# Attention scores as two fp32r passes over stacked halves, the residual parked in HBM, and transposes at later places

## The chip, the cores and the metric

The kernel runs on one core of a Trainium2 chip: TensorE (matrix products and transposes, PE in the profile, its weight loads PEld), VectorE (DVE), ScalarE (ACT), GpSimd (POOL), SyncE (SP), whose queue asks for the transfers, and 16 DMA engines. The metric is the time of one execution on the device in microseconds, as the median of several runs. A profile of one such execution shows every instruction of every engine; its time is counted over the span from its first to its last instruction.

## The reference

One layer of a decoder on 512 tokens of width 1024, all in fp32: two half-step SwiGLU feed-forward blocks, and between them a mixer in which a gated delta rule (four heads of 128) and a differential attention (four heads, two softmax maps of 64 dimensions each) stand side by side. Cut to what matters here:

```python
x = layer_norm(alpha * x + 0.5 * swiglu_ffn(x, ffn1_w13, ffn1_w2), ln1_g, ln1_b)
h = x @ w_in
gq, gk, gv, gz, ga, gb, dq, dk, dv = jnp.split(h, offsets, axis=-1)
y_a = gdn_mixer(gq, gk, gv, gz, ga, gb, ...)       # chunked delta rule, then RMS norm and a silu gate
y_b = diff_attention_mixer(dq, dk, dv, ...)
x = layer_norm(alpha * x + concatenate([y_a, y_b]) @ w_out, ln2_g, ln2_b)
ple = sigmoid(x @ ple_gate_w) * (p @ ple_proj_w)
x = layer_norm(alpha * x + 0.5 * swiglu_ffn(x, ffn2_w13, ffn2_w2) + ple, ln3_g, ln3_b)

# differential attention, one block of 128 queries
s = einsum("bqhmd,bkhmd->bhmqk", qb, k) * scale    # m: the two maps, d: 64
pr = softmax(where(q_pos >= k_pos, s, -inf))
attn = pr[:, :, 0] - lam * pr[:, :, 1]
y = rms_norm(einsum("bhqk,bkhd->bqhd", attn, v), subln_w) * (1 - lam_init)
```

## The kernel before

**Tiling.** The 512 tokens are four row blocks of 128, t = 0 to 3. The residual x lives in four tiles RES[t] of 128x1024 with tokens on the partitions; its transposed form, with the 1024 features on the partitions, is kept twice: XH, rounded to the narrower format fp32r, and XL, what the rounding left. Every weight is split in the same way, by a ScalarE cast (line 159) and a VectorE subtract (line 160). A product is then three fp32r passes, high by high, low by high and high by low (`mm3`, lines 297 to 299).

**First feed-forward block.** `ffn` ends (lines 604 to 624) with the second product of the last group, per row block t and half j. `natural(t)` is then the layer norm of the block (`norm_natural`, lines 302 to 334): statistics and most of the scaling on VectorE, the last 256 columns scaled by ScalarE and GpSimd (line 326 is GpSimd's last step). `norm_turn(t)` (lines 336 to 344) makes XH and XL of the block by eight transposes on TensorE. `turn(t - 1)` follows `natural(t)`; block 3 is turned within the next stage.

**Mixers.** `mix_zone` opens with values and gates, and the keys and queries of the delta rule. Then it weaves generators ("lanes"). Each yields a pair: the nominal TensorE cost of what it has just put into the program, and the time to wait before its next step; `weave` lets the first lane go on whose time has come. So the nominal numbers set the order of the program; a scheduler then sets that of each engine's queue, and every engine works its queue off in order. The lanes are: `gdn(c)`, the delta rule's inner work on four chunks; `diagonal`; `chain`, the state carried over the chunks; sixteen `attention(t, h)`, of which two are in flight at a time; `fill`, dense products (the attention's keys and queries and the remaining values and gates z) that stand between the others; `out_attn` and `out_gdn`, the output projection of either half of the mix.

**Attention.** `fill` makes the rotated keys and queries in natural form, transposes them (`turn4`, line 871) and a VectorE copy puts them into DKT and DQT, fp32 tiles with the 4 x 128 head dimensions on the partitions. A head (lines 1147 to 1188) then makes, for each of two maps, an fp32 product of 64 rows (line 1159), adds the causal mask by a bf16 product (line 1160), takes the row maximum (1161), the exponential (1164), weighs and adds the maps (1168), transposes the result (1172), copies it (1174), multiplies it with the values DV (1178) and norms the rows (1181 to 1186). Its result overwrites its queries in DQT; `to_mix` transposes it and splits it into XH and XL.

**Chain.** For each chunk, TensorE makes products with the state ST (lines 1205 and 1213), VectorE the new values (1207), TensorE a triangular solve's product (1220), ScalarE copies it (1222), TensorE the state's change (1230) and the output (1238), VectorE adds them (1235, 1241), ScalarE squares (1247), and VectorE scales four heads (1252).

**After the mixers.** `out_gdn` adds the projection to RES, norms each block and turns the one before; the second feed-forward stage (`second_ffn`) begins with the gate of the layer embedding and turns block 3 ahead of its t = 2.

## Time and profile before

| | us |
|---|---|
| median of 3 runs (1098.52 to 1100.03) | 1098.65 |
| the profiled execution | 1099.23 |
| its span, first to last instruction | 1097.4 |
| TensorE busy | 1068.6 (97%) |
| VectorE busy | 828.2 (75%) |
| ScalarE busy | 489.9 (45%) |
| GpSimd busy | 112.9 (10%) |

The span has these stretches: the first feed-forward block to 340 us, the norm and turn of its rows to 366, values, keys and queries to 478, the woven delta rule and attention heads to 612, chain and output projection to 667, its norms and turns to 700, and the second feed-forward block. A busy share is a mean over stretches with different limits, so each stretch is to be read by itself. A bracket behind a row of the timeline gives how long the engine stood before it, and what it had waited for. Matmuls are pipelined and their ends are modelled: the time that one takes in a row of many is read from start to start.

### The profile page before, as it was taken

The page shows a single profiled execution, that of the slowest core. Times are in us where ns is not written, and L with a number is a line of the kernel's source. Part 1 is how long each engine was busy: PE and PEld are TensorE (multiplying, and loading weights), DVE is VectorE, ACT ScalarE, POOL GpSimd, SP SyncE. Part 2 cuts the span into 40 slices and gives each one's busy share as a digit, 9 for nine tenths or more (in the row PEclk, how much of TensorE's full clock was granted, in tenths as well). Part 3 has the DMA queues.
Part 4 walks back from the last instruction along what each step waited for, and adds up shares of the span by engine and source line. Part 5 has one row for each costly group of instructions (what it writes and reads, how often), then busy time and mean ns, then how long its engine had stood idle before and what let it go on. Part 6 is the DMA issues. An engine that isn't in the chain of part 4 may idle for free.

```text
span 1097.4 us, 17374 instructions
## 1 busy us (share of the span) xinstructions
PE 1068.6 (97%) x6627; PEld 939.8 (86%) x6627; DVE 828.2 (75%) x1446; ACT 489.9 (45%) x948; POOL 112.9 (10%) x175
## 2 busy tenths in 40 slices
PE   9999999999999989999999999999999999999996
PEld 7889898989897978778865887779899998999895
DVE  5989796979678366356665658889989696979568
ACT  5745353535333356324365533545544353535231
POOL 1100000000002202432112213100000000000003
PEclk9999999999999999999999999999999999999999
DMA  8633332433242042123210201524343332433212
GB/s 293 202 110 116 103 109 77 117 107 104 77 136 77 1 135 80 36 78 87 58 39 20 77 16 62 163 87 135 101 131 97 106 106 78 118 112 97 77 39 96
DMA packets 44275, 106.03 MB, mean 97 GB/s; under 512 B 10848, under 2 KB 12528, under 8 KB 44192
## 3 DMA queue, kind: packets, MB, share of 16 engines
q1 hardware_dynamic: 37968, 96.71, 29.0%
q0 software_dynamic: 1808, 6.04, 1.7%
q10 hardware_dynamic: 4416, 2.16, 0.7%
q8 instruction: 52, 0.85, 0.3%
q14 instruction: 31, 0.25, 0.1%
HBM read 102.41 MB, written 2.49 MB: 96 GB/s over the span
## 4 chain that ended last, share of the span: by engine, by line
PE 55%; DVE 5%; POOL 2%; DMA 2%; ACT 2%; issue 1%; DVEq 0%; SPq 0%; ACTq 0%; POOLq 0%
PE pb L297 9%; PE pb L298 9%; PE pb L299 9%; PE pc L298 4%; PE pc L299 4%; PE pc L297 4%; PE pa L299 3%; PE pa L298 3%; PE pa L297 3%; PE pc L1159 2%; DMA raw<-in_wa_dram 2%; DVE wl L160 2%; ACT wh L159 1%; PE pa L1092 1%; PE pc L1178 1%
## 5 line engine op out<-in xcount | busy, mean ns | idle before, releaser
L160 DVE TENSOR_TENSOR wl<-raw,wh 128x1024 fp32r<-128x1024 f32 (+3 forms) x137 | 144.2, 1058 | 37.6 <-ACT wh L159 36.4
L159 ACT CAST wh<-raw 128x1024 fp32r<-128x1024 f32 (+3 forms) x137 | 123.2, 906 | 96.7 <-PE pa L298 30.7
L297 PE MATMUL pb<-wh,hh 128*128 128x512 f32 (+1 forms) x356 | 138.3, 389 | 3.7 <-DVE RES L807 1.5
L298 PE MATMUL pb<-wl,hh 128*128 128x512 f32 (+1 forms) x356 | 138.1, 388 | 0.0
L299 PE MATMUL pb<-wh,hl 128*128 128x512 f32 (+1 forms) x356 | 137.8, 387 | 0.0
L229 ACT CAST th<-tr 128x512 fp32r<-128x512 f32 x160 | 98.7, 620 | 83.4 <-PE pc L298 48.2
L233 DVE TENSOR_TENSOR tl<-tr,th 128x512 fp32r<-128x512 f32 x160 | 109.7, 687 | 11.0 <-ACT th L229 10.2
L190 ACT CAST wh<-raw 128x512 fp32r<-128x512 f32 x88 | 54.6, 623 | 135.1 <-PE pb L299 90.8
L297 PE MATMUL pb<-wh,XH 128*128 128x512 f32 (+2 forms) x288 | 110.8, 385 | 2.2 <-ACT wh L159 0.6
L298 PE MATMUL pb<-wl,XH 128*128 128x512 f32 (+2 forms) x288 | 106.1, 369 | 1.0 <-DVE wl L160 0.9
L299 PE MATMUL pb<-wh,XL 128*128 128x512 f32 (+2 forms) x288 | 105.9, 368 | 0.0
L298 PE MATMUL pa<-XL,wh 128*128 128x256 f32 (+1 forms) x344 | 100.0, 291 | 0.2 <-DVE XL L160 0.2
L297 PE MATMUL pa<-XH,wh 128*128 128x256 f32 (+1 forms) x344 | 100.0, 291 | 0.2 <-ACT wh L159 0.2
L299 PE MATMUL pa<-XH,wl 128*128 128x256 f32 (+1 forms) x344 | 99.9, 290 | 0.0
L297 PE MATMUL pc<-XH,th 128*128 128x256 f32 x320 | 90.6, 283 | 0.0
L298 PE MATMUL pc<-XL,th 128*128 128x256 f32 x320 | 90.6, 283 | 0.0
L299 PE MATMUL pc<-XH,tl 128*128 128x256 f32 x320 | 90.6, 283 | 0.0
L490 DVE TENSOR_TENSOR RES<-RES,pb 128x512 f32<-128x512 f32 (+1 forms) x81 | 54.6, 677 | 45.1 <-PE pb L299 44.4
L191 DVE TENSOR_TENSOR wl<-raw,wh 128x512 fp32r<-128x512 f32 x88 | 60.2, 691 | 32.2 <-ACT wh L190 32.0
L297 PEld LDWEIGHTS pb<-wh,hh 128*128 128x128 f32 x356 | 66.9, 188 | 19.4 <-DVE RES L807 1.8
L299 PEld LDWEIGHTS pb<-wh,hl 128*128 128x128 f32 x356 | 66.9, 188 | 13.7
L298 PEld LDWEIGHTS pb<-wl,hh 128*128 128x128 f32 x356 | 66.9, 188 | 13.2 <-DVE wl L191 0.3
(303 smaller groups left out, 2639.8 us busy)
## 6 DMA issues: line engine op xcount, KB each, us to landing
raw<-in_wa_dram SPq DMA_DIRECT2D x127, 512.0 KB, 3.7
raw<-in_wb_dram SPq DMA_DIRECT2D x88, 256.0 KB, 2.7
raw<-in_wd_dram SPq DMA_DIRECT2D x4, 520.0 KB, 3.7
RES<-in_xn_dram POOLq DMA_DIRECT2D x4, 512.0 KB, 6.3
gb<-in_gb_dram POOLq DMA_DIRECT2D x8, 256.0 KB, 3.9
xr<-in_xT_dram ACTq DMA_DIRECT2D x7, 256.0 KB, 4.4
out_dram<-RES SPq DMA_DIRECT2D x5, 256.0 KB, 2.1
TT<-in_gb_dram POOLq DMA_DIRECT2D x4, 256.0 KB, 3.6
```

Of the source, the lines that this page charges most:

```text
L159: return (self.nc.scalar.copy(hi, src), self.nc.vector.tensor_tensor(lo, src, hi.bitcast(F32), ALU.subtract))
L160: self.nc.vector.tensor_tensor(lo, src, hi.bitcast(F32), ALU.subtract))
L190: nc.scalar.copy(hi, r)
L191: nc.vector.tensor_tensor(lo, r, hi.bitcast(F32), ALU.subtract)
L229: act.copy(h, t)
L233: dve.tensor_tensor(hl[1], t, hl[0].bitcast(F32), ALU.subtract)
L297: pe.matmul(o, wh, xh, start=first, stop=False)
L298: pe.matmul(o, wh, xl, start=False, stop=False)
L299: pe.matmul(o, wl, xh, start=False, stop=last)
L490: dve.tensor_tensor(rj, rj, pd, ALU.add)
L1092: pe.matmul(pt[:, h * P:(h + 1) * P], MP[:, 0, c, h, :], TT[:, c, h, :], start=True, stop=True)
L1159: pe.matmul(sc[m], DQT[r, h, t * P:(t + 1) * P], DKT[r, h, 0:n], start=True, stop=False)
```

## The change

**Scores.** Keys are split. Each map m gets a tile KK[:, m] of 128 rows: the 64 rows of its own hold the high part of its keys, the 64 others the low part. A head first prepares its queries in a slot of QZ (four slots, used in turn): the high part of map m's queries on both halves of the rows, and a padded tile with their low part on the map's own rows and zeros on the others (zeroed once). Two fp32r passes over 128 rows then give high keys by high queries plus low keys by high queries, and high keys by low queries. The preparation is four ScalarE copies and two VectorE subtracts of 64x128 a head, with a yield of (0, 1.5) behind it; each key block takes two ScalarE copies and two VectorE subtracts of 64x512 where one VectorE copy was. The nominal cost of a head's scores falls from 0.2 + 0.43 (t + 1) to 0.1 + 0.24 (t + 1).

**Space.** The four residual tiles become one, RESA. During the mixers it is written to HBM (XR, four transfers of 512 KB on SP's queue after the third key head) and DQT and TT (a work tile of the delta rule) live in it. TT's zeroing on GpSimd moves from the zone's start to behind the keys. The blocks come back by four transfers: t = 2 and 3 when `out_attn` starts, t = 0 and 1 after all four `to_mix`. `out_attn` projects in the order 2, 3, 0, 1. The norm's gain and bias go to DV.

**Order.** The last key block's transposes are held until behind the first product of the queries. In the first block's end, `turn(0)` and `turn(1)` follow the products (2, 1) and (3, 0); blocks 2 and 3 are turned before the values of t = 1 and 2. In `out_gdn` block t - 2 is turned after the first half of t's projection; blocks 2 and 3 are turned behind the first two gate products of `second_ffn`.

```diff
@@ -123,7 +123,8 @@
...
         self.XL = cp.tile([P, KT, S], F32R, name="XL")
-        self.RES = [cp.tile([P, D], F32, name=f"RES{t}") for t in range(NT)]
+        self.RESA = cp.tile([P, NT, D], F32, name="RESA")
+        self.RES = [self.RESA[:, t] for t in range(NT)]
         self.CST = cp.tile([P, C_END], F32, name="CST")
@@ -615,13 +616,13 @@
...
                     cuts = [0, 512, 768, 1024]
+                if turn and (t, j) in ((2, 1), (3, 0)):
+                    turn(t - 2)
             natural(t, cuts, gbt)
...
                     self.ahead()
-            if turn and t:
-                turn(t - 1)
@@ -783,9 +784,9 @@
...
                         wp = [self.side(pp, f"wp{k}") for k in range(2)]
-                    if t == 2:
-                        self.norm_turn(NT - 1)
                     gate(t, 0, wg)
+                    if t < 2:
+                        self.norm_turn(NT - 2 + t)
                 for _ in range(2):
@@ -830,13 +831,15 @@
...
         MP = mp.tile([P, 2, NC, H, P], F32, name="MP")
-        TT = mp.tile([P, NC, H, P], F32, name="TT")
         UU = mp.tile([P, NC, H, P], F32, name="UU")
...
         DV = mp.tile([P, NT, H, P], F32, name="DV")
-        DKT = mp.tile([P, H, S], F32, name="DKT")
-        DQT = mp.tile([P, H, S], F32, name="DQT")
+        KK = mp.tile([P, 2, H, S], F32R, name="KK")
+        QZ = mp.tile([P, 4, 4, P], F32R, name="QZ")
+        DQT = [self.RESA[:, t // 2, (t % 2) * 512:(t % 2) * 512 + 512].rearrange("p (h b) -> p h b", b=P)
+               for t in range(NT)]
+        TT = self.RESA[:, 2:4].rearrange("p c (d h b) -> p (c d) h b", d=2, b=P)
         ST = [mp.tile([P, H, P], F32, name=f"ST{i}") for i in range(2)]
@@ -848,7 +851,7 @@
...
         DM, DT, DU = (dp.tile([NC, H, 8, 16, 16], F32, name=f"blocks{i}") for i in range(3))
-        pool.memset(TT, 0.0)
+        XR = dp.tile([NT, P, D], F32, name="XR")
         said = set()
@@ -912,8 +915,8 @@
...
             for t in range(NT):
-                if t == 2:
-                    self.norm_turn(NT - 1)
+                if t in (1, 2):
+                    self.norm_turn(NT - 3 + t)
                 tk = slice(t * P, (t + 1) * P)
@@ -976,6 +979,11 @@
...
                     held = (i, h)
+                    if i == 0 and h == 2:
+                        for t in range(NT):
+                            nc.sync.dma_start(XR[t], RES[t])
+                    if i == 1 and h == 0:
+                        pool.memset(TT, 0.0)
                     if i == 0 and h == 0:
@@ -992,15 +1000,25 @@
...
+        def rows(m):
+            return slice(m * DQK, (m + 1) * DQK)
         def fill():
-            for dst, word in ((DKT, "k"), (DQT, "q")):
+            held = None
+            for word in "kq":
                 w = [self.take() for _ in range(4)]
-                held = None
-                def turn(t, d):
+                def turn(word, t, d):
                     pt = ps("b")
                     turn4(pt, v4(d))
-                    dve.tensor_copy(dst[:, :, t * P:(t + 1) * P], v4(pt))
+                    if word == "k":
+                        for m in range(2):
+                            r, o = rows(m), rows(1 - m)
+                            hi = KK[r, m, :, t * P:(t + 1) * P]
+                            act.copy(hi, v4(pt)[r])
+                            dve.tensor_tensor(KK[o, m, :, t * P:(t + 1) * P], v4(pt)[r], hi.bitcast(F32), ALU.subtract)
+                    else:
+                        dve.tensor_copy(DQT[t], v4(pt))
                     said.add((word, t))
@@ -1009,15 +1027,15 @@
...
                             turn(*held)
+                    if word == "q" and t == 0:
+                        for m in range(2):
+                            pool.memset(QZ[rows(1 - m), :, 2 + m].bitcast(F32), 0.0)
                     d = tb()
...
                     rotary(d, t)
-                    held = (t, d)
+                    held = (word, t, d)
                 yield 0, 0
-                last = held
-                if word == "k":
-                    turn(*last)
-                    yield 0.5, 0
+            last = held
             held = last
@@ -1145,7 +1163,17 @@
         def attention(t, h):
             n = (t + 1) * P
+            i = (t * H + h) % 4
+            qz = QZ[:, i]
+            for m in range(2):
+                r, o = rows(m), rows(1 - m)
+                act.copy(qz[r, m], DQT[t][r, h])
+                act.copy(qz[o, m], DQT[t][r, h])
+                dve.tensor_tensor(qz[r, 2 + m], DQT[t][r, h], qz[r, m].bitcast(F32), ALU.subtract)
+            yield 0, 1.5
             if t < 2:
@@ -1155,8 +1183,8 @@
...
             for m in range(2):
-                r = slice(m * DQK, (m + 1) * DQK)
-                pe.matmul(sc[m], DQT[r, h, t * P:(t + 1) * P], DKT[r, h, 0:n], start=True, stop=False)
+                for q in (m, 2 + m):
+                    pe.matmul(sc[m], qz[:, q], KK[:, m, h, 0:n], start=q == m, stop=False)
                 pe.matmul(sc[m][:, n - P:n], idb, negb, start=False, stop=True)
@@ -1166,7 +1194,7 @@
...
             dve.scalar_tensor_tensor(pr[0], pr[1], rr[:, 1:2], pr[0], ALU.mult, ALU.add)
-            yield 0.2 + 0.43 * (t + 1), 4.5 + 0.8 * t
+            yield 0.1 + 0.24 * (t + 1), 4.5 + 0.8 * t
             pt = ps("c")
@@ -1176,7 +1204,7 @@
...
                 pe.matmul(po[:, 0:P], at[:, c * P:(c + 1) * P], DV[:, c, h, :], start=c == 0, stop=c == t)
-            y = DQT[:, h, t * P:(t + 1) * P]
+            y = DQT[t][:, h]
             so = stat([P, 4], "aso")
@@ -1259,15 +1287,15 @@
...
-        def project_out(w, half, t):
+        def project_out(w, half, t, js=(0, 1), last=NT - 1):
             tk = slice(t * P, (t + 1) * P)
-            for j in range(2):
+            for j in js:
                 pd = ps("b")
...
                         w[k][1][:, j * 512:(j + 1) * 512], k == 0, k == 3)
-                    if t == NT - 1 and j == 1:
+                    if t == last and j == 1:
                         self.ahead()
@@ -1277,25 +1305,30 @@
...
         def out_attn():
+            for t in (2, 3):
+                nc.sync.dma_start(RES[t], XR[t])
             for t in range(NT):
-                to_mix(DQT[:, :, t * P:(t + 1) * P], t, 4, "c")
+                to_mix(DQT[t], t, 4, "c")
                 yield 0.5, 0
+            for t in (0, 1):
+                nc.sync.dma_start(RES[t], XR[t])
             w = [self.take() for _ in range(4)]
-            for t in range(NT):
-                yield from project_out(w, 0, t)
+            for t in (2, 3, 0, 1):
+                yield from project_out(w, 0, t, last=1)
             said.add("out_attn")
         def out_gdn():
-            gbt = [TT[:, j].rearrange("p a b -> p (a b)") for j in range(4)]
+            gbt = [DV[:, j].rearrange("p a b -> p (a b)") for j in range(4)]
             self.load_gb(gbt, G_LN2)
...
                     yield 0, 0.5
-                yield from project_out(w, 1, t)
+                for j in range(2):
+                    yield from project_out(w, 1, t, (j,))
+                    if j == 0 and t > 1:
+                        self.norm_turn(t - 2)
                 self.norm_natural(t, LN_EPS, gbt)
-                if t:
-                    self.norm_turn(t - 1)
```

Line numbers of the changed kernel: `mm3` 298 to 300, `norm_turn` 342, `turn4` 874, scores 1187, mask 1188, transposes of the weights 1200, value product 1206, chain 1233, 1241, 1248, 1258 and 1266.

Three places show what this moves in TensorE's queue. The first is the end of the first feed-forward block, before: L341 are the transposes of block 0 (RES_69), the others products of blocks 2 and 3.

```order
L297 MATMUL pb_3960<-wh_3829,hh_3275 128x512
L298 MATMUL pb_3960<-wl_3830,hh_3275 128x512
L299 MATMUL pb_3960<-wh_3829,hl_3276 128x512
L297 MATMUL pb_3960<-wh_3838,hh_3563 128x512
L298 MATMUL pb_3960<-wl_3839,hh_3563 128x512
L341 MATMUL pa_3932<-CST,RES_69 128x128 x4
L341 MATMUL pa_3939<-CST,RES_69 128x128 x4
L299 MATMUL pb_3960<-wh_3838,hl_3564 128x512
L297 MATMUL pb_3960<-wh_3847,hh_3695 128x512
L298 MATMUL pb_3960<-wl_3848,hh_3695 128x512
L299 MATMUL pb_3960<-wh_3847,hl_3696 128x512
```

The transposes of block 0 stand five products into block 2's second half, right behind its norm. After (L342, RESA):

```order
L298 MATMUL pb_3943<-wh_3844,hh_3692 128x512
L299 MATMUL pb_3943<-wl_3845,hh_3692 128x512
L300 MATMUL pb_3943<-wh_3844,hl_3693 128x512
L298 MATMUL pb_3943<-wh_3851,hh_3781 128x512
L299 MATMUL pb_3943<-wl_3852,hh_3781 128x512
L300 MATMUL pb_3943<-wh_3851,hl_3782 128x512
L342 MATMUL pa_3957<-CST,RESA 128x128 x4
L342 MATMUL pa_3964<-CST,RESA 128x128 x4
L298 MATMUL pb_3987<-wh_3411,hh_3272 128x512
L299 MATMUL pb_3987<-wl_3412,hh_3272 128x512
L300 MATMUL pb_3987<-wh_3411,hl_3273 128x512
```

The whole of block 2's last product group now stands ahead of them.

The second place is where the z-gate products end, before. L297 to L299 on pb_6229 are the last of them, L1220 to L1238 the chain's first chunk, L871 the transposes of attention outputs into the mix, and pb_6370 is the first output product.

```order
L299 MATMUL pb_6229<-wh_5849,XL 128x512
L1220 MATMUL pa_6293<-VV,UU 128x128 x2
L871 MATMUL pc_6300<-CST,DQT 128x128 x4
L871 MATMUL pc_6307<-CST,DQT 128x128 x4
L871 MATMUL pc_6337<-CST,DQT 128x128 x4
L1230 MATMUL pa_6314<-ta_6298,KD 128x128 x4
L1238 MATMUL pa_6320<-ta_6298,MP 128x128 x4
L871 MATMUL pc_6344<-CST,DQT 128x128 x4
L1205 MATMUL pa_6351<-ST_4080,KQ 128x128 x4
L1213 MATMUL pa_6361<-ST_4080,KQ 128x128 x4
L297 MATMUL pb_6370<-wh_5957,XH 128x512
L298 MATMUL pb_6370<-wl_5958,XH 128x512
```

All heads are done here, and from the first output product on twelve such rows stand between any two groups of the chain. After, L300 on pb_6130 is the last z product:

```order
L300 MATMUL pb_6130<-wh_5786,XL 128x512
L1248 MATMUL pa_6222<-VV,UU 128x128
L1187 MATMUL pc_6167<-KK,QZ 128x384 x2
L1188 LDWEIGHTS idb
L1188 MATMUL pc_6167<-LVM,idb 128x128
L1200 MATMUL pc_6229<-CST,tt_6150 128x128 x3
L1258 MATMUL pa_6235<-ta_6227,KD 128x128 x4
L1266 MATMUL pa_6241<-ta_6227,MP 128x128 x4
L1206 MATMUL pc_6258<-DV,tt_6233 128x128 x3
L1200 MATMUL pc_6269<-CST,tt_6170 128x128 x3
L1233 MATMUL pa_6281<-ST_4062,KQ 128x128 x4
L1241 MATMUL pa_6291<-ST_4062,KQ 128x128 x4
```

The chain's first chunk (L1248, L1258, L1266) now lies among the scores, transposes and value products of heads, with no dense product between.

The third place is the end of that stretch, where before twelve products stood between the last groups of the chain, and after, L874 are the transposes into the mix and pb_6669 and pb_6683 the first output products:

```order
L1206 MATMUL pc_6599<-DV,tt_6577 128x128 x4
L874 MATMUL pa_6611<-CST,ta_6567 128x128 x4
L1200 MATMUL pc_6618<-CST,tt_6583 128x128 x4
L1206 MATMUL pc_6625<-DV,tt_6623 128x128 x4
L874 MATMUL pc_6639<-CST,RESA 128x128 x4
L874 MATMUL pc_6646<-CST,RESA 128x128 x4
L874 MATMUL pc_6653<-CST,RESA 128x128 x4
L874 MATMUL pc_6660<-CST,RESA 128x128 x4
L298 MATMUL pb_6669<-wh_5900,XH 128x512
L299 MATMUL pb_6669<-wl_5901,XH 128x512
L298 MATMUL pb_6683<-wh_5900,XH 128x512
```

The output products now come behind the last head and the last transposes, 156 in a row.

## Rows read from the trace of the kernel before

**Rows 1.** The page, part 1: busy time, share of the span, instructions.

```profile
PE 1068.6 (97%) x6627; PEld 939.8 (86%) x6627; DVE 828.2 (75%) x1446; ACT 489.9 (45%) x948; POOL 112.9 (10%) x175
```

**Rows 2.** Windows by stage; the columns are named in the first line.

```profile
core 0: us, PE busy (x) PEld busy (x) DVE busy (x) ACT busy (x) POOL busy (x), PEclk, DMA share, GB/s
...
340.00:366.00 26.00, 23.10 (x135) 19.58 (x134) 23.33 (x47) 6.46 (x13) 13.63 (x17) 1.00 0.15 41
366.00:478.00 112.00, 107.51 (x557) 88.72 (x558) 53.51 (x88) 50.75 (x128) 27.24 (x38) 1.00 0.26 77
478.00:612.00 134.00, 131.78 (x726) 98.07 (x726) 84.11 (x222) 64.97 (x154) 26.57 (x57) 1.00 0.16 45
612.00:667.00 55.00, 53.11 (x311) 44.91 (x310) 34.60 (x71) 22.79 (x67) 9.59 (x10) 1.00 0.26 77
```

**Rows 3.** Timeline, PE: scores and mask, t=0, t=3. Start, us, engine, line, operation, tiles, shapes.

```profile
484.06 0.48 PE L1159 MATMUL pc<-DKT,DQT 64*128 64x128 f32 x2
484.48 0.23 PE L1160 MATMUL pc<-LVM,idb 128*128 128x128 bf16 x1
...
580.16 1.12 PE L1159 MATMUL pc<-DKT,DQT 64*128 64x512 f32 x2
581.22 0.23 PE L1160 MATMUL pc<-LVM,idb 128*128 128x128 bf16 x1
```

**Rows 4.** Timeline, PE: 256 columns fp32r, 128-column transposes, chain groups, 512 columns fp32r.

```profile
364.97 0.28 PE L297 MATMUL pb<-wh,XH 128*128 128x256 f32 x1
365.09 0.28 PE L298 MATMUL pb<-wl,XH 128*128 128x256 f32 x1
...
531.91 0.60 PE L1172 MATMUL pc<-CST,tt 128*128 128x128 f32 x4
532.35 0.28 PE L1108 MATMUL pa<-UU,ta 128*128 128x128 f32 x1
...
620.42 1.06 PE L1205 MATMUL pa<-ST,KQ 128*128 128x128 f32 x8
621.32 1.06 PE L1213 MATMUL pa<-ST,KQ 128*128 128x128 f32 x8
...
622.44 0.39 PE L298 MATMUL pb<-wl,XH 128*128 128x512 f32 x1
622.67 0.40 PE L299 MATMUL pb<-wh,XL 128*128 128x512 f32 x1
```

**Rows 5.** Timeline, ACT and DVE: a table load, exponentials, a square, a copy, four scalings.

```profile
600.08 1.28 ACT L1164 ACT_TABLE_LOAD   x1
601.38 0.69 ACT L1164 ACTIVATE tt<-pc,amx 128x512 f32<-128x512 f32 x1
...
602.63 0.20 ACT L1164 ACTIVATION_READ_ACCUMULATOR pc<-pc,amx 128x1 f32 x1
...
619.83 0.27 ACT L1247 ACTIVATE VV<-pa 128x128 f32<-128x128 f32 x1
...
626.12 0.59 ACT L1222 COPY ta<-pa 128x512 f32<-128x512 f32 x1 [2.57 <-PE pa L1220]
...
622.27 1.13 DVE L1252 SCALAR_TENSOR_TENSOR ta<-pa,gso,MP 128x128 f32<-128x128 f32 x4 [1.13 <-POOL gso L1249]
```

**Rows 6.** Waits of PE (us in total, times, longest), and the timeline of its longest.

```profile
PE pa L341 <- POOL RES L326: 3.6, 4, 1.3
...
346.76 0.82 PE L341 MATMUL pa<-CST,RES 128*128 128x128 f32 x6
348.86 0.44 PE L341 MATMUL pa<-CST,RES 128*128 128x128 f32 x2 [1.28 <-POOL RES L326]
```

**Rows 7.** Timeline, PE: the transposes of the last key block.

```profile
472.09 0.66 PE L871 MATMUL pb<-CST,tb 128*128 128x128 f32 x4 [1.59 <-POOL tb L910]
```

**Rows 8.** Timeline, PE: a stand in the chain, and one ahead of a score.

```profile
617.47 0.94 PE L1230 MATMUL pa<-ta,KD 128*128 128x128 f32 x6 [0.43 <-ACT ta L1222]
...
601.52 1.12 PE L1159 MATMUL pc<-DKT,DQT 64*128 64x512 f32 x2 [0.52 <-DVE DQT L1186]
```

## What I predicted before the run

> **What bounds the kernel now.** I read the page's busy shares first, then the same shares stage by stage, and only then single stretches of the timeline. TensorE is busy 97% of the span [rows 1], so what the change does to TensorE's queue is what counts. By stage [rows 2]: in the stretch of the heads (478 to 612 us) it is busy 131.78 of 134 us, in that of the chain and the first output products (612 to 667) 53.11 of 55, while VectorE and ScalarE have half or a third of their time free. In the short stretch where the first FFN's rows are normalised (340 to 366) VectorE is busy 23.33 of 26 us and TensorE stands for 2.9. So time comes out of this kernel in two ways: by fewer TensorE microseconds, or by filling the stands. It is lost wherever TensorE's queue holds nothing that is ready.
>
> **The change, part by part.** The sum is made against the profiled execution (1099.23 us; its span is 1097.4) and then set on the median, 1098.65. A price of TensorE is taken from start to start, since ends are modelled and neighbours overlap.
>
> 1. *Score passes.* One map of a head with t=0 takes 0.42 us for its score and its mask, with t=3 1.06 [rows 3]: 0.64 us for three further blocks of 128 key columns, 0.21 each, so 0.63 for t=1 and 0.84 or 0.85 for t=2. There are eight maps of each t: before, 8 x (0.42 + 0.63 + 0.84 + 1.06) = 23.6 us. After, each map has two fp32r passes of 128 rows. Such a product of 512 columns follows the one before it by 0.23 us and one of 256 columns by 0.12 [rows 4]; 384 lies between at 0.17. An fp32r pass of 128 columns has no row. The transposes of 128 columns go at 0.44/4 = 0.11 each [rows 4], and the fp32 score of 128 columns with its mask at 0.42 leaves 0.21 as the top. I take 0.11, because 256 columns need no more than 0.12. So 16 x (0.11 + 0.12 + 0.17 + 0.23) = 10.1 us, and the part gives **-13.5 us** (-11.9 with 0.21).
>  Its price lies on the other engines: per head four ScalarE copies and two VectorE subtracts of 64x128, and per key turn two of each of 64x512 for one VectorE copy. The nearest rows for the small ones are 0.27 for a 128x128 activation on ScalarE and 1.13/4 = 0.28 for four 128x128 operations on VectorE [rows 5], which bound them from above, nothing from below: at most 1.6 us a head. Heads run woven into dense products, with VectorE at 84 and ScalarE at 65 of 134 us [rows 2], so I book nothing. That cover is gone for the last five heads (part 4), and there it is in the sum.
>
> 2. *Later transposes.* Four times TensorE reaches the last two transposes of a 128-row block before GpSimd has scaled their columns: 3.6 us in the waits, with 1.28 us for the longest [rows 6]. The next start is late by 1.44 us there, since the bracket leaves out what a modelled end covers: 0.16 a stand. So 3.6 + 4 x 0.16 = 4.2 us. In the changed order a whole product group of 12 matmuls or more lies between a block's normalisation and its transposes, and at the change of stages two whole row blocks. GpSimd and VectorE do no more than before; they only get later deadlines. **-4.2 us**, or 0 if VectorE, 23.33 of 26 us busy, falls behind by as much as it gains.
>
> 3. *Held key turn.* The last transposes of the key block wait 1.59 us for the rotary on GpSimd [rows 7]; now the query block's first product stands ahead of them. 1.59 + 0.16 = **-1.7 us**.
>
> 4. *The tail of the mixers.* This is the term that the order decides. Before, the z-gate products reach to the last head, and then 12 output products stand between any two steps of the delta-rule chain: 12 x 0.23 = 2.8 us of cover while VectorE and ScalarE do the next link. After, the score passes are cheaper, the weave gives out its products sooner, the last of them stands ahead of the second map of head (2,3), and the output products come as one row of 156 behind the last head. So one map, four whole heads, the chain's remaining steps and the transposes into the mix stand on TensorE with only each other as cover.
>  TensorE's own work there: 17 chain groups of eight rows at about 0.89 (0.90 in [rows 4]) 15.1 us; nine score maps 4.3; 28 transposes and as many value products in two rows each 2.4 and 4.9; 16 + 16 transposes of output blocks 3.6. Together 30.3 us.
>  I then followed the three queues by hand in the new order, each step with a row of the old trace: two exponentials 1.45 from the start of the first to the end of the second's read, an activation table load 1.28, a copy 0.59, four scalings 1.13 [rows 5], and the like. From the end of the last z product the state products of the three chunks start at 5.6, 14.9 and 25.2 us, the last output of the chain at 35.2, the last head's value product at 45.7; its scaled rows are there at 48.6, and the transposed ones with their high and low parts at 50.7. The pace, about 10 us a chunk with its head, is that of VectorE, for which my list adds to 7.7 us a chunk and head, with the handovers to ScalarE (5.8) and TensorE (7.5) between. So TensorE stands for 50.7 - 30.3 = **+20.4 us**. The bounds: nothing, if the three queues interlock without a gap (30.3 us); and about 33, if nothing at all overlaps but TensorE's own products: to the 30.3 us come three chunks with their heads at VectorE's 7.7 us each, and one head more at 10 (63 us). I take the hand count; it lies between them because the new order alternates between a head and a chunk, and each covers a part of the other.
>
> 5. *Stands that lose their place.* In 612 to 667 five stands of the old weave end (the first of them in [rows 8]; the five brackets are 0.43, 0.41, 0.46, 0.23 and 0.27): 1.80 + 5 x 0.16 = **-2.6 us**. Two stands at the old t=3 heads, 0.52 + 0.16 [rows 8] and one like it, lie within part 4's count now: **-1.4 us**.
>
> 6. *Residual out and back.* Eight transfers of 512 KB on SP's queue. Stores leave after the third key head; the zeroing of TT on GpSimd now waits for them, with the delta-rule masks behind it on that engine. Moving DMA stands at 0.26 of its capacity there [rows 2]. The rows of t=2 and 3 are asked for long before use, those of t=0 and 1 behind all transposes, with 78 products (18 us) before their first use. I book nothing; if the cover were short, one transfer, a few microseconds, would be late.
>
> The sum: -13.5 - 4.2 - 1.7 + 20.4 - 2.6 - 1.4 = -3.0. The profiled run would take 1096.2 us, its span 1094.4, the median **1095.6 us**.
>
> **The rivals.** (A) is this forecast; its own range, with part 1 at either price and the tail at 47 to 55 us, is 1091 to 1100.
> (B) *The tail interlocks better.* VectorE's 7.7 us a chunk and four of them make 31 us, about TensorE's own 30.3; a tail of 40 us gives 1098.65 - 3.0 - 10.7 = 1085. For it: VectorE and ScalarE are free for half of the stage [rows 2]. Against it: each link of the chain and of a head is a handover.
> (C) *Slower, by the new step at the head's start.* Scores can't start before copies and subtracts of their own queries, which stand on ScalarE behind exponentials and weight splits, on VectorE behind maxima and splits of 1 us. Place: the first score of each of 16 heads. TensorE's queue goes in order, so every product behind it waits too. Price: 0.5 us a head makes +8, 1103.6. It decides from 0.33 us a head (5.2 / 16), from which the result is slower. For it: a stand of 0.52 at a score is there already [rows 8]. Against it: the weave asks for 1.5 us of other work behind the new step, and two heads are in flight.
> (D) *ScalarE runs empty at each table load.* In the trace a load takes 1.28 us and the next activation starts 0.02 us after its end [rows 5], so the sum has no more for it. The tail has two loads with nothing to hide them, for exponentials and for the gate's function. If ScalarE stood as long again at each, the time would be 1095.6 + 2 x 1.28 = 1098.2, no change. The Trainium skill (ScalarE: Activation LUTs, What ACT_TABLE_LOAD costs) counts a drain of 1.38 us with every switch of the table set, which by its figure would be an estimate of 2.8 us; the trace doesn't agree, by the 0.02 us above.
> (E) *The transposes stand all the same,* because VectorE is the bound of the stage: 1095.6 + 4.2 = 1099.8.
> (F) *The clock falls.* All stretches show a granted clock of 1.00, that is 2.4 GHz, with TensorE busy for at least 23.10 of 26 us [rows 2]. The new tail has it busy for 30 of 51. If the clock went to 1.2 GHz in it, half of its TensorE work over again, some 13 us as far as it lies on the path, comes on top: 1108. For it, only that no stretch of the old trace is as sparse; against it, that none shows a fall.
>
> **How the numbers follow.** 0.2% of the time, 2.2 us, is about what a measurement of this kernel can tell: faster is below 1096.45, slower above 1100.85. Chances: A 0.45, of it 0.30 faster, 0.14 the same, 0.01 slower; B 0.20, faster; C 0.16, slower; D 0.07 and E 0.07, the same; F 0.05, slower. Together 0.50 faster, 0.28 the same, 0.22 slower. The likeliest case gives 1095.6. From 1084 to 1104 leaves out nearly half of B, F and the worse part of C, some 0.2.
>
> **What would show it.** Score products in pairs 0.11 to 0.23 us apart (part 1). No stand of TensorE for GpSimd at the transposes (2), nor behind the key block (3). Between the last z product and the first of the 156 output products, 47 to 55 us with TensorE busy for 30, the state products about 10 us apart, and stands ended by VectorE and ScalarE in turn (4). The granted clock there tells F; a stand of over 0.3 us before most first scores, ended by the copies or subtracts of the queries, tells C. The forecast is wrong if the tail is under 46 or over 56 us, or if TensorE's stands in 478 to 612 grow by more than the 2.2 us they have.

## The result, and the profile after

The changed kernel takes 1106.24 us as the median of four runs (1106.02 to 1107.30), the kernel before beside it 1098.59 (1098.30 to 1100.03). The ratio is 1.007, with a 95% interval of 1.0057 to 1.0083: 7.6 us slower, where 3.0 us faster was forecast, and above the upper end of the range, 1104. The profiled execution took 1107.30 us, its span 1105.5 (before: 1099.23 and 1097.4).

First the busy shares of the page, which answer to [rows 1]:

```profile
PE 1063.4 (96%) x6627; PEld 946.2 (86%) x6627; DVE 836.0 (76%) x1482; ACT 514.0 (46%) x1021; POOL 110.3 (10%) x177
```

TensorE is busy for 5 us less and the span is 8 longer. So 13 us of new stands have come, and some of the busy time is slow. Where, the windows of [rows 2] show (the same columns: length, busy time of the engines, granted clock, DMA):

```profile
340.00:366.00 26.00, 24.45 (x147) 21.15 (x146) 23.41 (x48) 6.71 (x14) 14.39 (x19) 1.00 0.32 113
366.00:478.00 112.00, 106.93 (x549) 87.37 (x547) 57.04 (x93) 55.07 (x136) 27.21 (x37) 1.00 0.27 79
478.00:612.00 134.00, 123.54 (x744) 105.50 (x745) 89.17 (x244) 85.30 (x215) 24.36 (x51) 0.96 0.21 61
612.00:667.00 55.00, 47.16 (x260) 38.47 (x259) 28.65 (x75) 21.61 (x70) 8.44 (x16) 0.94 0.11 39
```

Two things are to be seen: TensorE's busy time falls by 8 and 6 us in the heads' and the chain's stretches, and their clock is no longer 1.00. Windows cut at the changed kernel's own marks tell more: the tail, from the last z product (it starts at 590.67, and 590.90 is one pitch of 0.23 later) to the first output product (644.26); the output projection up to the second feed-forward block; and three stretches within which the clock is low.

```profile
590.90:644.30 53.40, 39.51 (x257) 32.95 (x255) 33.38 (x100) 33.73 (x106) 14.04 (x23) 0.87 0.14 41
644.30:706.80 62.50, 60.76 (x272) 47.72 (x273) 39.94 (x64) 16.18 (x22) 13.16 (x16) 1.00 0.29 93
479.20:482.60 3.40, 3.40 (x9) 2.62 (x8) 1.51 (x8) 0.00 (x0) 0.92 (x3) 0.50 0.15 39
595.00:602.00 7.00, 4.84 (x21) 4.47 (x22) 2.41 (x6) 4.66 (x11) 2.47 (x3) 0.52 0.37 108
636.00:643.00 7.00, 5.00 (x21) 4.23 (x22) 1.80 (x6) 1.86 (x5) 2.31 (x5) 0.52 0.18 54
```

The waits of TensorE (us in total, times, longest) name the new stands; the transposes' wait for GpSimd, 3.6 us in [rows 6], is down to 0.3. Three of the lines are of the scores (L1187), and none of them names the copies or subtracts of a head's queries:

```profile
PE pc L1200 <- DVE tt L1196: 4.1, 2, 2.4
PE pb L298 <- ACT tb L1034: 2.3, 1, 2.3
PE pa L1258 <- ACT ta L1250: 2.2, 2, 1.9
PE pc L1187 <- DVE amx L1189: 2.0, 1, 2.0
PE pc L1187 <- DVE RESA L1214: 1.7, 3, 0.8
PE pc L1187 <- ACT tt L1192: 1.5, 1, 1.5
PE pb L298 <- ACT AB L931: 1.2, 1, 1.2
PE pa L342 <- POOL RESA L327: 0.3, 1, 0.3
```

To place the loss, the same dense product can be followed in both traces; each has 5820 of them in one order. Starts in us:

| dense product | before | after | difference | forecast |
|---|---|---|---|---|
| 2351st, within the values | 375.21 | 373.98 | -1.2 | -2.9 |
| 2601st, within the delta rule's keys and queries | 431.66 | 430.56 | -1.1 | -2.9 |
| 2751st, within the attention's queries | 481.23 | 483.32 | +2.1 | -4.6 |
| 3000th, the last z product | 614.89 | 590.67 | -24.2 | -31 |
| 3241st, the first of the second block | 698.28 | 706.80 | +8.5 | -3.0 |
| 5820th, the last | 1088.39 | 1096.44 | +8.1 | -3.0 |

So 5 of the 11 us that are missing were lost at the key and query blocks, 1 to 2 at the end of the first block, and nearly 5 between the last z product and the second block. Between the 2751st and the last z product, where the heads are woven into products, the difference falls by 26.3 us, as the forecast's terms make it: the maps, transposes and value products that the order moves behind the last z product 16.6, cheaper scores of the others 8.5, two stands 1.4, together 26.5. That the two agree so closely is partly luck: the stand of 2.0 us at a first head, ended by VectorE's maxima (line 1189), is new there and in no term.

**The query block.** Here are ScalarE's rows and then TensorE's at the last key block (start, us, engine, line, operation):

```profile
474.76 0.58 ACT L1018 CAST KK<-pb 64x512 fp32r<-64x512 f32 x1 [4.53 <-PE pb L874]
475.24 1.90 ACTq L1136 DMA_DIRECT2D blocks<-MP  x4
477.18 0.58 ACT L1018 CAST KK<-pb 64x512 fp32r<-64x512 f32 x1 [1.83 <-issue]
477.78 0.59 ACT L1034 COPY tb<-pb 128x512 f32<-128x512 f32 x1
```

```profile
475.72 0.40 PE L300 MATMUL pb<-wh,XL 128*128 128x512 f32 x1
478.42 0.50 PE L298 MATMUL pb<-wh,XH 128*128 128x512 f32 x1 [2.30 <-ACT tb L1034]
478.75 0.39 PE L299 MATMUL pb<-wl,XH 128*128 128x512 f32 x1
478.98 0.43 PE L300 MATMUL pb<-wh,XL 128*128 128x512 f32 x1
479.22 0.62 PE L298 MATMUL pb<-wh,XH 128*128 128x512 f32 x1
479.64 0.63 PE L299 MATMUL pb<-wl,XH 128*128 128x512 f32 x1
```

The key block now needs two copies by ScalarE. Between them ScalarE issues the four transfers of the delta rule's diagonal blocks (1.90 us); the copy that empties the first query block's PSUM tile stands behind the second, and TensorE has nothing to write to: the next product starts 2.70 us after the one before it, where 0.23 is the pitch [rows 4], a stand of 2.47 us. Then products follow each other by 0.42 instead of 0.23 for 3.4 us, at a granted clock of 0.50, that is 1.2 GHz: 8 x 0.2 = 1.6 us more. In the kernel before the same four issues were over at 476.94, the copy of the first query block came at 478.31, and TensorE has no stand behind it:

```profile
473.90 3.04 ACTq L1118 DMA_DIRECT2D blocks<-MP  x4
478.31 0.59 ACT L1013 COPY tb<-pb 128x512 f32<-128x512 f32 x1 [8.32 <-DMA blocks<-MP]
```

What the clock cost here can be told apart from the stand. One of the kernels below, with the chain behind the last head, has the same order on TensorE up to this place; it has the same stand, and the clock stays at 1.00 behind it:

```profile
476.65 0.50 PE L298 MATMUL pb<-wh,XH 128*128 128x512 f32 x1 [2.30 <-ACT tb L1034]
...
476.60:480.00 3.40, 3.35 (x15) 2.78 (x16) 0.85 (x6) 0.00 (x0) 1.62 (x5) 1.00 0.13 39
```

From the 2601st to the 2751st product it takes 51.0 us, the changed kernel 52.8, the kernel before 49.6. So of the 3.2 us lost there 1.7 are the clock, and 1.5 are the rest, the stand above all.

**The tail** is as the order had told: 53.4 us, where 50.7 were counted by hand. In its two slow windows TensorE is busy for 4.84 and 5.00 us; at full clock that is half, so the clock cost 4.9 us at most, and some 4 is my estimate. The same two groups of the chain, eight rows each, stand here in the slow stretch and one chunk later at full clock:

```profile
598.01 2.07 PE L1258 MATMUL pa<-ta,KD 128*128 128x128 f32 x8 [1.93 <-ACT ta L1250]
599.88 1.92 PE L1266 MATMUL pa<-ta,MP 128*128 128x128 f32 x8
...
609.16 1.16 PE L1258 MATMUL pa<-ta,KD 128*128 128x128 f32 x8 [0.29 <-ACT ta L1250]
610.15 1.06 PE L1266 MATMUL pa<-ta,MP 128*128 128x128 f32 x8
```

1.87 us from start to start in the first, 0.99 in the second.

### The profile page after: what moved, and what is told of

Its sections match the earlier page's. It is cut to its first block, busy times and chain, and to the rows that moved or that the text cites. A ratio compares the mean times of both kernels' runs of the same rounds, so it can differ in the third digit from the quotient of the medians.

```text
span 1105.5 us, 17508 instructions
## 1 busy us (share of the span) xinstructions
PE 1063.4 (96%) x6627; PEld 946.2 (86%) x6627; DVE 836.0 (76%) x1482; ACT 514.0 (46%) x1021; POOL 110.3 (10%) x177
## 4 chain that ended last, share of the span: by engine, by line
PE 49%; DVE 8%; ACT 4%; DMA 3%; POOL 2%; issue 2%; ACTq 0%; DVEq 0%; SPq 0%; POOLq 0%
PE pb L298 8%; PE pb L299 8%; PE pb L300 8%; PE pc L299 4%; PE pc L300 4%; PE pc L298 4%; PE pa L299 3%; PE pa L300 3%; DMA raw<-in_wa_dram 3%; PE pa L298 3%; DVE wl L161 2%; ACT wh L160 1%; DVE tb L900 1%; PE pa L1110 1%; PE pc L1187 1%
## 5 line engine op out<-in xcount | busy, mean ns | idle before, releaser
L299 PE MATMUL pb<-wl,hh 128*128 128x512 f32 (+1 forms) x356 | 138.0, 388 | 0.0
L300 PE MATMUL pb<-wh,hl 128*128 128x512 f32 (+1 forms) x356 | 137.8, 387 | 0.0
L299 PE MATMUL pb<-wl,XH 128*128 128x512 f32 (+2 forms) x288 | 107.0, 372 | 1.5 <-DVE wl L161 1.3
L300 PE MATMUL pb<-wh,XL 128*128 128x512 f32 (+2 forms) x288 | 106.1, 369 | 0.0
L299 PE MATMUL pa<-XL,wh 128*128 128x256 f32 (+1 forms) x344 | 100.0, 291 | 0.7 <-DVE XL L161 0.7
L300 PE MATMUL pa<-XH,wl 128*128 128x256 f32 (+1 forms) x344 | 100.0, 291 | 0.0
L299 PE MATMUL pc<-XL,th 128*128 128x256 f32 x320 | 90.6, 283 | 0.0
L300 PE MATMUL pc<-XH,tl 128*128 128x256 f32 x320 | 90.6, 283 | 0.0
L491 DVE TENSOR_TENSOR RESA<-RESA,pb 128x512 f32<-128x512 f32 (+1 forms) x81 | 54.6, 677 | 45.2 <-PE pb L300 44.4
L300 PEld LDWEIGHTS pb<-wh,hl 128*128 128x128 f32 x356 | 66.9, 188 | 13.8
L299 PEld LDWEIGHTS pb<-wl,hh 128*128 128x128 f32 x356 | 66.9, 188 | 13.2 <-DVE wl L192 0.3
```

Source lines behind the costliest of these rows:

```text
L299: pe.matmul(o, wh, xl, start=False, stop=False)
L300: pe.matmul(o, wl, xh, start=False, stop=last)
L491: dve.tensor_tensor(rj, rj, pd, ALU.add)
```

## The experiments

Each ratio is against the kernel before, run on the same chip, with its 95% interval. The changed kernel stands at 1.0070 (1.0057 to 1.0083).

### The diagonal blocks' transfers from another queue

```diff
-                (nc.scalar if b % 2 else nc.sync).dma_start(
+                nc.sync.dma_start(
                     DM[:, :, b].rearrange("c h j i -> j (c h) i"), MP[r, 0, :, :, r].rearrange("j c h i -> j (c h) i"))
```

> The changed kernel, and only the queue of four transfers changed: the delta rule's diagonal blocks are all sent from SyncE's queue, where four of eight were sent from ScalarE's. In the changed kernel ScalarE stands behind these four issues (1.90 us) with the copy of the last key block's second map and then the copy of the first query block, TensorE stands 2.47 us at 478.42, and the clock is at 1.2 GHz until 482.6 (eight products 0.42 apart, some 1.7 us). Theory A (the issues on ScalarE's queue make the stand, the stand makes the slow clock): both go, 1106.2 - 4.2 = 1102. Theory B (the last key block would be late anyway, through GpSimd's rotary and the split into two parts): the stand stays, 1106 within 0.5.

Measured: 1106.86 us, ratio 1.0089 (1.0073 to 1.0106). No gain. The stand at the query block falls from 2.70 to 1.61 us from start to start and the clock stays up; the 2751st product starts 2.8 us earlier than in the changed kernel, counted from the 2601st. But at the heads that follow there are two stands that the changed kernel didn't have:

```profile
475.60 0.50 PE L298 MATMUL pb<-wh,XH 128*128 128x512 f32 x1 [1.22 <-ACT tb L1034]
...
499.34 0.50 PE L298 MATMUL pb<-XH,wh 128*128 128x512 f32 x1 [0.93 <-ACT tb L1034]
...
504.00 0.44 PE L1187 MATMUL pc<-KK,QZ 128*128 128x128 f32 x2 [1.05 <-DVE amx L1189]
```

So the issues on ScalarE's queue made 1.1 us of the stand's 2.5, less than theory A had it. The rest stays with the key block's two copies: the second waits 0.75 us for VectorE's first subtract. Theory B has the time about right, but not for its reason: 2.8 us are won ahead of the first heads, and 2.3 of them are lost again between the 2751st and the last z product.

### The key block's transposes back at their place

```diff
                 yield 0, 0
+                if word == "k":
+                    turn(*held)
+                    held = None
+                    yield 0.5, 0
             last = held
```

> The changed kernel with the last key block's transposes back at their place of before, directly behind its rotary. The forecast booked 1.7 us of gain for holding them: undone, 1.0085 of the kernel before. By the trace after, holding them made a stand of 2.47 us and a slow clock worth 1.7, against the old stand of 1.75: undone, 2.4 us less, 1.005. Theory B (what is gained ahead of the first heads comes back in new stands at them, as with the issues moved to SyncE): as the changed kernel, 1.007.

Measured: 1108.35 us, 1.0094 (1.0079 to 1.0109): 2.6 us more than the changed kernel, nearer to the forecast's 1.7 than to the gain which the trace after had made me expect. The trace doesn't bear the forecast's reason out. The old stand comes back larger than in [rows 7], 2.14 us, with a slow clock behind it, and the 2751st product is where it was within 0.7 us, counted from the 2601st; the time is lost at the heads, in stands of 1.5 us at 508 and 2.4 us at 551 (a slow clock behind this one) that the other order doesn't have. In this kernel holding the transposes neither won nor lost at its own place.

### All transposes of normalised rows back at their places

```diff
-                if turn and (t, j) in ((2, 1), (3, 0)):
-                    turn(t - 2)
...
+            if turn and t:
+                turn(t - 1)
...
+                    if t == 2:
+                        self.norm_turn(NT - 1)
                     gate(t, 0, wg)
-                    if t < 2:
-                        self.norm_turn(NT - 2 + t)
...
-                if t in (1, 2):
-                    self.norm_turn(NT - 3 + t)
+                if t == 2:
+                    self.norm_turn(NT - 1)
...
-                    if j == 0 and t > 1:
-                        self.norm_turn(t - 2)
                 self.norm_natural(t, LN_EPS, gbt)
+                if t:
+                    self.norm_turn(t - 1)
```

> The changed kernel with every transpose of normalised rows back at its place of before (both feed-forward ends and the output projection). The forecast booked 4.2 us for the later places: 1110.4. By the trace after, the first group gained only 1.6 (the copies of the values wait for the last norm step, whatever the transposes do), the second about 1: 1108 to 1109. If the places are worth nothing: 1106.

Measured: 1108.27 us, 1.0101 (1.0083 to 1.0119): 3.4 us more than the changed kernel, with 2 or so to either side. By the same products in the traces it is about 1.5 us at the first block's end and 0.7 at the second's. The later places are a gain, smaller than 4.2.

### One fp32 pass in the place of two

```diff
-                for q in (m, 2 + m):
-                    pe.matmul(sc[m], qz[:, q], KK[:, m, h, 0:n], start=q == m, stop=False)
+                r = rows(m)
+                pe.matmul(sc[m], qz[r, m].bitcast(F32), KK[r, m, h, 0:n].bitcast(F32), start=True, stop=False)
...
-            yield 0.1 + 0.24 * (t + 1), 4.5 + 0.8 * t
+            yield 0.2 + 0.43 * (t + 1), 4.5 + 0.8 * t
```

> The changed kernel with the two fp32r passes of a map replaced by one fp32 pass of 64 rows over the high parts, and the nominal cost of before; the low parts are prepared but left out of the scores, so the output lacks them. TensorE has 13.5 us of scores more. Theory A (the passes do save their 13.5 us, but the order gives most of it back in the tail): about 8.5 us more where heads are woven into products, little in the tail, since its stands take it up: 1110 to 1116. Theory D (the saving is lost entirely, since heads are bound by their own chain): 1105 to 1108.

Measured: 1109.13 us, 1.0113 (1.0096 to 1.0130): only 4.7 us more than with the two passes by the ratios, which set on the changed kernel's 1106.2 is 1111, at the lower end of theory A's band and above theory D's. The last z product starts 9.3 us later, counted from the 2601st, and the tail is 4.2 us shorter: of what the passes save, a third was left.

### No step between preparation and scores

```diff
                 dve.tensor_tensor(qz[r, 2 + m], DQT[t][r, h], qz[r, m].bitcast(F32), ALU.subtract)
-            yield 0, 1.5
             if t < 2:
```

> The changed kernel without the yield of (0, 1.5) between a head's preparation and its scores; what is computed is the same. In the order 4 score passes, 8 transposes and 12 value products are left behind the last z product, where the changed kernel has 18, 22 and 22. Theory A (the step puts the heads back in the weave, two heads behind when the delta rule's inner work takes TensorE, and this makes the long tail with 23 us of stands and two of the three slow clocks): the tail from the last z product to the last value product falls from 50 to under 20 us, the time by 10 to 18, to 1088 to 1096. Theory C (the score passes wait for their queries: the preparation needs the cover that the step asks for): stands of 0.5 us or more at most of the 16 heads eat 8 of that, 1098 to 1104. Theory D (the tail is only moved, the heads are bound by their own chain): 1104 to 1107.

Measured: 1094.74 us (1091.12 to 1097.07 in ten runs), 0.9971 (0.9958 to 0.9985). One line of the nominal times is worth 1.0%, some 11 us. The trace bears out what the order had shown: from the last z product to the last value product it takes 13 us, not 50, and to the first output product 21.1, not 53.6:

```profile
478.00:604.90 126.90, 118.86 (x700) 98.41 (x700) 87.70 (x245) 81.57 (x208) 23.41 (x48) 0.98 0.17 50
604.90:626.00 21.10, 17.96 (x137) 16.77 (x136) 15.61 (x37) 16.51 (x46) 9.29 (x12) 0.92 0.54 162
```

The stand of 2.3 us at the query block is still there, and its slow clock. In the stretch of the heads TensorE stands for 8 us; the longest stands, 3.2 and 2.2 us, are transposes that wait for ScalarE's silu of the values and GpSimd's rotary. Only one, of 0.47 us, waits for a head's own queries, so theory C isn't seen.

### The same, with the transfers moved

The two edits shown above together.

> The run without the step between preparation and scores, and with the diagonal blocks sent from SyncE's queue. In the run without the step the stand at the query block (2.47 us) and its slow clock (about 1.8 us) were still there. Theory A (time is additive, since the heads now end with the products): both go, 4 us less, 0.993 of the kernel before. Theory B (as in the run that moved only the issues, the time comes back in new stands at the first heads, since ScalarE and VectorE are what these heads wait for): 0.997 as without.

Measured: 1097.40 us, 1.0002 (0.9992 to 1.0013): 3.4 us worse than without the second edit. Both theories missed. The stand at the query block is shorter again and its slow clock gone, but two stands of 2.3 and 2.4 us stand behind the last z product (610 and 615 us), where the run without the edit has one of 2.4. By the traces 2.6 us are won up to the 2751st product, and 5.5 are lost from there to the second block. My reading is that an edit ahead of the heads shifts which of their steps meet on ScalarE; no run shows it apart.

### Preparation once for four heads

```diff
-            i = (t * H + h) % 4
-            qz = QZ[:, i]
-            for m in range(2):
-                r, o = rows(m), rows(1 - m)
-                act.copy(qz[r, m], DQT[t][r, h])
-                act.copy(qz[o, m], DQT[t][r, h])
-                dve.tensor_tensor(qz[r, 2 + m], DQT[t][r, h], qz[r, m].bitcast(F32), ALU.subtract)
-            yield 0, 1.5
+            qz = QZ[:, h]
+            if h == 0:
+                for m in range(2):
+                    r, o = rows(m), rows(1 - m)
+                    act.copy(QZ[r, :, m], DQT[t][r])
+                    act.copy(QZ[o, :, m], DQT[t][r])
+                    dve.tensor_tensor(QZ[r, :, 2 + m], DQT[t][r], QZ[r, :, m].bitcast(F32), ALU.subtract)
+                said.add(("qz", t))
...
+            if h:
+                need.add(("qz", t))
+            elif t:
+                need |= {("sc", t - 1, g) for g in range(H)}
```

> The changed kernel with the queries of all four heads of a row block prepared at once, by four ScalarE copies and two VectorE subtracts of 64x512 instead of sixteen and eight of 64x128, and without the step; the first head of a block then waits until the scores of the block before are asked for. Theory E (the preparation's own cost matters: sixteen copies of 0.30 us against four of about 0.58 a block, 2.5 us less of ScalarE and 1 of VectorE in each of four blocks): 3 us or more below the run without the step, 0.994 or less. Theory A (only its place in the weave matters): 0.996 to 0.999.

Measured: 1100.05 us, 1.0027 (1.0017 to 1.0037). ScalarE has less to do and the time is 6 us above the run without the step: a cheaper preparation by itself bought nothing (theory E), and theory A's number was missed as well. The edit also makes a block's heads wait for each other, and no run separates the two. The longest stands are 3.8 us for ScalarE's silu of the values and 2.8 us for the rotary.

### The chain behind the last head

```diff
-                pe.matmul(po[:, 0:P], at[:, c * P:(c + 1) * P], DV[:, c, h, :], start=c == 0, stop=c == t)
+                self.lastv = pe.matmul(po[:, 0:P], at[:, c * P:(c + 1) * P], DV[:, c, h, :], start=c == 0, stop=c == t)
...
-                for h in range(H):
-                    pe.matmul(px[:, h * P:(h + 1) * P], UU[:, c, h, :], R[:, h, :], start=True, stop=True)
+                with self.behind([self.lastv] if c == 0 else []):
+                    for h in range(H):
+                        pe.matmul(px[:, h * P:(h + 1) * P], UU[:, c, h, :], R[:, h, :], start=True, stop=True)
...
-        need_chain = {("gdn", c) for c in range(NC)} | {"v", "z"}
+        need_chain = {("gdn", c) for c in range(NC)} | {"v", "z"} | {("attn",) + th for th in heads[:16]}
```

> The changed kernel, but the chain starts only behind the last head's value product, so that it has the output products between its steps as before, while the last heads stand alone. Heads alone: the last heads need some 28 us from the last z product (two pairs of 12 and the remainder), then 72 products' worth of cover for the chain. Theory A (the tail is long because heads and chain share VectorE and ScalarE, 10 us a chunk): tail and chain together 116 - 6 = 110 us from the last z product to the second block, 1.001 of the kernel before. Theory D (the heads' own chain sets the tail, the chain of the delta rule was free in it): the chain's time comes on top, 1.010 or more.

Measured: 1111.38 us, 1.0127 (1.0109 to 1.0144). Theory D's side: from the last z product to the last value product the heads alone take 39 us, where heads and chain together took 50, and the chain comes on top. The window from the last z product to the first output product:

```profile
588.90:634.30 45.40, 30.44 (x151) 24.39 (x150) 20.64 (x59) 23.96 (x63) 9.93 (x19) 0.70 0.21 64
```

VectorE and ScalarE are idle for half of it, so they are not the bound; each link waits for the one before. The sparse stretch also has the clock at half for most of it, 0.70 in the mean, so the heads' 39 us are not a time at full clock.

### Attention ahead in the weave, three heads in flight

```diff
-            if i >= 2:
-                need.add(("attn",) + heads[i - 2])
+            if i >= 3:
+                need.add(("attn",) + heads[i - 3])
...
-        lanes += [Lane(attention(*th), attn_ready(i)) for i, th in enumerate(heads)]
+        lanes = lanes[:1] + [Lane(attention(*th), attn_ready(i)) for i, th in enumerate(heads)] + lanes[1:]
```

> The changed kernel, step kept, but the attention lanes stand ahead of the delta rule's in the weave and three heads may be in flight. In the order no score pass, transpose or value product is left behind the last z product, and the chain has the output products between its steps again. Theory A (the tail is what costs, whatever makes it): as with the step taken out or better, 0.990 to 0.998 of the kernel before. Theory D (heads are bound by ScalarE, VectorE and three PSUM tiles: a third head in flight only waits, with TensorE behind it): 1.000 to 1.007.

Measured: 1090.61 us, 0.9942 (0.9926 to 0.9959), theory A. The step is kept; the last value product ends at 580, ahead of the last z product (606.7), and six microseconds lie between the latter and the first output product. Which of the two edits does it, the place in the weave or the third head, was not tried:

```profile
478.00:607.00 129.00, 123.22 (x740) 103.20 (x739) 90.46 (x262) 78.11 (x214) 23.00 (x55) 0.98 0.20 55
607.00:613.00 6.00, 5.88 (x52) 5.64 (x51) 4.19 (x5) 5.48 (x16) 3.52 (x3) 1.00 0.88 315
```

### The same order with one fp32 pass

> The kernel with the attention lanes ahead and three heads in flight (no tail), with one fp32 pass of 64 rows over the high parts in the place of the two fp32r passes, and the nominal cost of before; the low parts are left out of the scores. It measures what the score passes are worth where no tail gives it back. Part 1 of the forecast right (13.5 us of TensorE on the path): 1090.6 + 13.5, 1.0065 of the kernel before. If heads are bound by ScalarE and VectorE, and the saving falls into stands: 0.994 to 0.999.

Measured: 1106.12 us, 1.0073 (1.0058 to 1.0088), 1.3% or 14.4 us above the run with the two passes (some 2.5 to either side). In the traces the stretch from 478 us to the last z product grows from 129.0 to 143.4 us:

```profile
478.00:621.40 143.40, 138.93 (x742) 105.83 (x743) 92.77 (x262) 75.69 (x212) 26.52 (x59) 0.96 0.17 50
```

About 1 us of that is a longer slow clock. Where no tail takes it back, the saving of the passes is on the path in full.

### The same order in the kernel before

> The kernel before, with only the order of the run of that name: attention lanes ahead in the weave, three heads in flight. Theory A (that order repairs a tail which only the changed kernel has): 0.997 to 1.003 of the kernel before. Rival (the order is a gain of its own, and the whole change is worth nothing beside it): 0.990 to 0.995.

Measured: 1098.70 us, 1.0009 (0.9998 to 1.0020): nothing. The kernel before had no tail, so the order has nothing to repair there. The gain of 0.6% and the loss of 0.7% are both the changed kernel's.

### The same order in the changed kernel, with the key turn back

> The kernel with the attention lanes ahead and three heads in flight, and the last key block's transposes back at their place of before. In the run without this the stand of 2.47 us at the query block and 4 us of slow clock (2 us) were there, and a stand of 1.83 us at the first heads. Theory A: the first two go, the old stand of 1.75 comes back, 2.5 us less: 0.992 of the kernel before. Theory B (time ahead of the first heads comes back at them): 0.994.

Measured: 1087.17 us (1087.00 to 1089.35), 0.9908 (0.9892 to 0.9925): 10 us under the kernel before, the fastest of all and on theory A's side. Against the same order with the turn held that is 3.4 us, so here the gain ahead of the heads is passed on. The clock stays at 1.00 from the first head to the last z product:

```profile
478.00:603.70 125.70, 119.79 (x736) 100.81 (x735) 88.08 (x262) 78.22 (x214) 24.98 (x58) 1.00 0.20 57
```

## Why the prediction was wrong

**What held.** The reading of the order held: the tail without products came where it was forecast, with its length (53.4 against 50.7 us) and its pace (the chain's products of line 1258 start at 7.1, 18.3 and 28.0 us after the last z product, forecast 5.6, 14.9 and 25.2). What stood for a gain did gain: the score passes, which are shown by the fp32 pass in the order without a tail (14.4 us, forecast 13.5), and the later transposes. By the rows the passes save somewhat less. Two maps of 512 columns follow each other like this:

```profile
621.02 0.71 PE L1187 MATMUL pc<-KK,QZ 128*128 128x512 f32 x2
621.58 0.23 PE L1188 MATMUL pc<-LVM,idb 128*128 128x128 bf16 x1
621.62 0.71 PE L1187 MATMUL pc<-KK,QZ 128*128 128x512 f32 x2
```

0.60 us a map, where 2 x 0.23 = 0.46 was booked, against 1.06 in [rows 3]. The two passes take 0.56: with the change from one kind of product to another they need 0.1 us more than two pitches. The mask takes the other 0.04; the sum had it in the price before and left it out after. In the tail's sum the transposes and value products are 22 each and not 28; its 2.4 and 4.9 us are right for 22.

**Step 3, the held key turn, failed.** -1.7 us was booked; up to the 2751st product the change had instead lost 3.2 us since the 2601st, 4.9 us off and the largest part of the 11 that are missing: 1.7 of slow clock and 1.5 of the new stand and what goes with it, where a wait of 1.7 was to go. My step looked at the wait that goes (GpSimd's rotary) and not at what the same edit puts behind ScalarE: with two copies a key block, ScalarE's queue became the way by which TensorE's PSUM tile is emptied, and four issues of transfers stood in that queue. In the kernel before TensorE did not wait behind these issues. The run that moved them shows that they made 1.1 us of the stand's 2.5. In the order without a tail, holding the turn costs 3.4 us (1090.61 against 1087.17). In the changed kernel itself, repairing the stand changed no time and undoing the hold made it 2.6 us slower; that its 5 us are lost for good is not shown there, they are only where the loss stands in this trace.

**Step 2 was too large.** 4.2 us booked, about 1.5 + 0.7 seen in the traces of the run that undoes it, 3.4 in its time. At the end of the first block the values' first products were sooner at hand, but ScalarE can't empty their PSUM tile until the last block's norm is done: 1.2 us in the waits above (AB, line 931), 0.4 before. A transpose was late; with that gone, the next reader of the same norm is.

**The clock, rival F, came true in part.** I gave 0.05 to it, as 13 us and 1108. It fell three times before the last dense product, for 17 us in all, and cost some 1.6 us behind the query block and 4 (an estimate, at most 4.9) in the tail. The forecast's tail was priced at full clock throughout; this is enough for its 2.7 us over. That the median, 1106, came near F's 1108 is chance: F put all its 13 us into the tail.

**Rival D** fell too. In the tail a load stands just behind the last z product, and the exponential follows at once:

```profile
590.81 1.28 ACT L1192 ACT_TABLE_LOAD   x1
592.11 0.58 ACT L1192 ACTIVATE tt<-pc,amx 128x384 f32<-128x384 f32 x1
```

0.02 us lie between, as in [rows 5]. The drain of 1.38 us that the Trainium skill (ScalarE: Activation LUTs, What ACT_TABLE_LOAD costs) counts with each switch isn't there in this trace.

**The output projection** was 2 us longer than the forecast's terms 2 and 5 left it: TensorE stands five times in this stretch, 1.4 us by the brackets, for the splits of weights on VectorE (0.17, 0.17 and 0.22) and ScalarE (0.54) and for a residual sum (0.32). That 156 products in a row want their weights faster is my reading of it.

**What lies behind the loss as a whole.** The forecast added up places, as if each stretch's gain were passed on. In the two runs that moved the issues it wasn't: my reading is that the heads are a chain of short links, and the time is set by when they start and how many are in flight. The step with its nominal 1.5 us put the weave two heads back by the time that the delta rule's inner work took TensorE over. The fifth head's scores start at 540.26 us in the trace after and at 517.99 without the step:

```profile
540.26 0.48 PE L1187 MATMUL pc<-KK,QZ 128*128 128x256 f32 x2
...
517.99 0.48 PE L1186 MATMUL pc<-KK,QZ 128*128 128x256 f32 x2
```

In the trace before they start at 508.41. By 537 us four heads have begun in the trace after, six without the step; and behind the last z product four whole heads and a map are left in the first, one head in the second. Without the step 11 us go, with the heads ahead of the delta rule and three in flight the tail goes and with it 14 us. The order after showed me the tail, and I priced it about right; I took it for a property of cheaper scores, while it came mostly from one number. Rival B, a shorter tail by a better interlock, didn't come. Rival C, scores that wait for their own queries, didn't either: no wait of the scores names the queries' copies or subtracts. E fell with the 0.3 us of wait that is left at the transposes.

**What stays open.** Why moving the issues helps nothing with the step and harms without it was seen in the stands, which moved; no run separates it from chance in the order. How much of the 7.6 us is the clock alone was not tried apart: 5 to 6 us by the rows, of which the 1.7 behind the query block are borne out by the same stand at full clock. The transfers of the residual were in no wait of TensorE; they were not left out in any run.

## What to carry to other kernels

When a change makes an engine's work cheaper within an order that was woven by nominal times, the saved time is real only if the latency-bound lanes move forward with it: follow in the order where the last of them ends against the last filling product, before and after, and if a tail comes up, look first for the number that put it there. Count what an edit adds to each queue that frees a buffer, issues of transfers too; a wait that goes at one reader turns up at the next reader of the same result. And try the order on the old kernel as well: it tells whether the order or the change is the gain.

## What the runs showed of the hardware

Ahead of the last product the granted clock fell 31 times in the fourteen traces, 29 times in or close behind a stand of 1.4 us or more; but the stand alone doesn't decide. The stand of 2.0 us at a first head of the changed kernel, at 490.85, has a clock of 1.00 behind it. And here is the same stand, at the same place, before the same products, in two kernels:

```profile
470.15 0.66 PE L874 MATMUL pb<-CST,tb 128*128 128x128 f32 x4 [2.14 <-POOL tb L913]
470.56 0.68 PE L298 MATMUL pb<-wh,XH 128*128 128x512 f32 x1
471.04 0.63 PE L299 MATMUL pb<-wl,XH 128*128 128x512 f32 x1
```

```profile
470.46 0.66 PE L874 MATMUL pb<-CST,tb 128*128 128x128 f32 x4 [2.12 <-POOL tb L913]
470.88 0.48 PE L298 MATMUL pb<-wh,XH 128*128 128x512 f32 x1
471.19 0.39 PE L299 MATMUL pb<-wl,XH 128*128 128x512 f32 x1
```

The first is the changed kernel with the key turn back: the products behind the stand are 0.42 us apart, at 1.2 GHz. The second has the attention lanes ahead and three heads in flight besides: 0.23 apart, at 2.4 GHz. The rows ahead of the stand, eight products of line 1096, are the same in both. Stretches at the lower clock lasted from 3 to 10 us in these runs, and one sparse stretch of 45 us, with TensorE busy for 30, had it for most of its length.

Four issues of transfers took 1.90 us of ScalarE's queue (3.04 in the kernel before), and nothing else of that queue moved meanwhile.
